# High weights of layer 1's paired units, placed 64 bytes lower in four tiles of their own

## The chip, the cores and the metric

The kernel runs on one core of one Trainium2 chip. The metric is the device time of one execution in microseconds (us); a run gives one time, and the median of several runs is compared.

A core has five engines that matter here: TensorE (PE in the profile, with its weight loads as PEld), VectorE (DVE), ScalarE (ACT), GpSimd (POOL) and SyncE (SP), which issues most of the DMA transfers. They run side by side and meet at semaphores. Data is worked on in a memory of 128 partitions; a tile takes the same bytes of each partition, and its address is the byte at which it starts there. A matmul has a stationary operand of 128 columns (the weights), which is loaded into the array first, and a moving operand of up to 512 columns, which streams past it.

## The reference

Two layers of a transformer-like mixer on 256 latent and 256 context tokens, 2048 features wide, in float32:

```python
for l in range(DEPTH):                                   # DEPTH = 2
    shift, scale, gate = jnp.split(silu_c @ w_mod[l] + b_mod[l], 3, axis=-1)
    h = rmsnorm(x, g_pre[l]) * (1.0 + scale[:, None]) + shift[:, None]
    h_c = rmsnorm(ctx, g_pre[l]) * (1.0 + scale_c) + shift_c
    proj, proj_c = h @ w_in[l], h_c @ w_in[l]
    y = mixer_branches(proj, latent_attn, ...)           # gMLP, attention, Fourier, each with a gate
    x_new = x + gate[:, None] * rmsnorm(y @ w_out[l], g_post[l])
    if not last:
        ...                                              # the same for the context
```

`w_in[l]` is 2048 by 5120 and `w_out[l]` 2048 by 2048. The second layer needs of the context only the keys and values, since only the latent tokens are returned.

## The kernel before

**Float32 in two parts.** Each operand of a large matmul is split into a high part (a cast to the type float32r) and a low part (the rest). A product of two operands is then three matmuls: high by high, high by low, low by high (`mm3`, L575).

**The stream of weights.** The weights come in chunks of 128 partitions by 1024 float32, 4096 bytes on each partition. The class `Stream` (L471) lists them in the order of use. For each one, SP issues the load into a tile `raw` (a ring of three), ACT casts it to `whi` (L544) and DVE writes the rest to `wlo` (L546). Both `whi` and `wlo` are rings of four tiles: the allocator gives the next chunk a tile whose last reader is done, and the cast waits for that reader. The stream runs three chunks ahead of the matmuls (`AHEAD`). Chunks that stand in `place` go to other tiles, and the two chunks of the unit `v` hold high and low parts of half a chunk in each tile (`twins`, L549).

**The units.** A unit is 128 columns of `w_in` by all 2048 rows: 16 blocks of 128 rows, in two chunks. In layer 0, `tunit` (L718) runs `mm3` for each block over the 512 columns of both streams of tokens. In layer 1 the tiles `hh` and `hl` hold, for latents and context in turn, high and low part side by side, 256 columns each. There `tunit1` (L742) runs a pair for each block (`mm2`, L730): the high weight against all 512 columns (L732), and the low weight against the 256 columns of the high part (L733). `joined` adds the two halves of the result. Units in pairs are `au2`, `au3`, `cx`, `ag`, `cg` (four each), `k` (two, each with both streams), `q` and `bg` (eight each); `av`, `au01` and `v` of layer 1 are worked in other ways.

**The order.** TensorE's instructions stand in the order in which the code issues them. Other work (attention, Fourier, the conditioning sums on DVE) is cut in steps and put between the matmuls by a planner of due times (`Later`). DVE, ACT and SP are ordered by a scheduler from priorities.

**Homes.** At the start `HOMES` (L93) creates one tile of every large tag in a fixed order, so that each has a fixed address; tags that aren't listed follow in the order of their first use. All homes but three at the start (`ct`, `cs`, `gs0`, 128 bytes each) and the last, `kt0`, take multiples of 512 bytes. `ones` is a tile of 128 by 128 ones; matmuls read up to 32 of its columns, and L1333 casts it all to a float32r tile for the last stage.

Of the kernel before, what the change touches and what calls it, by code (L numbers as in the profile page):

```python
# [7 lines left out]
F32 = mybir.dt.float32  # L8
F32R = mybir.dt.float32r
# [4 lines left out]
P = 128  # L14
D = 2048
KT = D // P
S = 256
# [49 lines left out]
def trunk_kernel(ctx: ExitStack, tc: tile.TileContext, xT, xhalf, cT, wss, wsl, wmod, win, wout0, wout1, const, vec, rows,  # L67
                 wmat, bs, sink, out):
    nc = tc.nc
    V, A, G, PE, DMA = nc.vector, nc.scalar, nc.gpsimd, nc.tensor, nc.sync  # L70
# [6 lines left out]
    def sb(shape, dt, tag, bufs=1):  # L77
        cnt[0] += 1
        return pool.tile(shape, dt, tag=tag, bufs=bufs, name=f"{tag}_{cnt[0]}")

    def w2k(shape, dt=F32):
        return sb(shape, dt, "w2k", W2K)
# [5 lines left out]
    def ms_ps(name="ms"):  # L88
        cnt[0] += 1
        return psum.tile([P, 512], F32, tag="ms", bufs=2, name=f"ps_{name}_{cnt[0]}")  # L90


    HOMES = ([("ct", 32, 1), ("cs", 32, 1), ("gs0", 32, 1)] + [(f"yy{i}", 1024, 1) for i in range(8)]  # L93
             + [("join", 256, 2), ("w2k", 512, W2K), ("mraw", 1024, 2)]
             + [(tag, 1024, n) for tag, n in (("macc", 1), ("vv", 1), ("raw", 3), ("whi", 4), ("wlo", 4), ("mg", 1), ("mgl", 1))]
             + [(f"{tag}{i}", 512, 1) for i in range(KT) for tag in ("hh", "hl")]
             + [(tag, 512, 1) for tag in ("acc", "ctrh", "ctrl", "nstrh", "nstrl", "ws", "bsb", "kt1")]
             + [("identr", P, 1), ("ones", P, 1), ("red", P, 2), ("m0r", P, 1), ("rbs", S, 2), ("kt0", 2 + KT * 32, 1)])
    for tag, n, bufs in HOMES:
        sb([P, n], F32, tag, bufs)  # L100

# [9 lines left out]
    ct = sb([P, KT, 2], F32, "ct")  # L111
    vecs = sb([P, 2, NVEC], F32, "vecs")
    cst = sb([P, NKEEP - P], F32, "cst")
    ones = sb([P, P], F32, "ones")
    V.memset(ones, 1.0)
    mhalf8 = sb([P, 8], F32, "mhalf")
    mhalf = mhalf8[:, 0:4]
# [19 lines left out]
    class low:  # L137


        def __init__(self, n):  # L140
            self.n = n
# [16 lines left out]
    identr = sb([P, P], F32R, "identr")  # L158
# [5 lines left out]
    gg0 = sb([P, KT, 2], F32, "gg0")  # L164
# [223 lines left out]
    state = {"ctx": [], "phase": "", "owed": 0.0}  # L388
# [43 lines left out]
    class Later:  # L432
# [19 lines left out]
        def flush(self):  # L452
# [6 lines left out]

    OUT = list(range(8, KT)) + list(range(8))  # L460
    NHI, NLO, NRAW = 4, 4, 3
    TAIL = [(("hl0 hl1", 1), ("hl2 hl3", 1)), (("hl4 hl5", 1), ("hl6 hl7", 1)),
            (("mraw", 2), ("mraw", 2)), (("macc", 1), ("ws bsb", 1)),
            (("yy4", 1), ("yy5", 1)), (("yy6", 1), ("yy7", 1))]
# [6 lines left out]
    class Stream:  # L471
        AHEAD = 3

        def __init__(self):
            self.src, self.out, self.pos, self.stop = [], [], 0, 0
            self.raws, self.rest = [], []
            self.place, self.behind, self.twin = {}, {}, set()
            for l in range(2):
                def half(name, i, h):
                    return win[l, UIDX[name][i], h]  # L480
                for i in range(2):
                    a = [half("av", 2 * i, 0), half("au01", i, 0), half("av", 2 * i, 1),
                         half("av", 2 * i + 1, 0), half("au01", i, 1), half("av", 2 * i + 1, 1)]
                    if l == 0:
                        a.insert(3 - i, half("au2", 0, i))
                        self.place[len(self.src) + 3 - i] = AU2[i]
                    self.src += a
                for i, u in enumerate(UNITS):
                    if u[0] not in ("av", "au01") + ("au2",) * (l == 0):
                        if u[0] == "v":  # L490
                            self.twin.update((len(self.src), len(self.src) + 1))
                        self.src += [win[l, i, 0], win[l, i, 1]]
                if l == 0:
                    self.src += [wout0[j, i] for j in OUT for i in range(2)]
                else:
                    self.src += [wout1[c, i] for c in range(4) for i in range(8)]
                if l == 0:
                    n = len(self.src) - 2 * HELD
                    self.place[n] = (("mraw", 2), ("mraw", 2))
                    self.place[n + 1] = (("macc", 1), ("mg", 1))  # L500
            for i, tags in enumerate(TAIL):
                self.place[len(self.src) - len(TAIL) + i] = tags
            self.raw_place = {len(self.src) - len(TAILRAW) + i: tags for i, tags in enumerate(TAILRAW)}
# [16 lines left out]
        def load_rest(self):  # L520
            n, r = self.rest.pop(0)
            DMA.dma_start(r[:, 512:], self.src[n][:, 512:])

        def emitting(self, cut=1024):

            if len(self.raws) == len(self.out):
                self.load()
            n = len(self.out)
            r = self.raws[n]
            if n in self.twin:  # L530
                yield from self.twins(r)
                return
            tags = self.place.get(n, (("whi", NHI), ("wlo", NLO)))
            hi, lo = ([sb([P, 1024 // len(t[0].split())], F32R, tag, t[1]) for tag in t[0].split()] for t in tags)
            self.out.append((hi, lo))
            cut = min(cut, 1024 // max(len(hi), len(lo), len(r) if isinstance(r, list) else 1))
            for i in range(0, 1024, cut):
                c = slice(i, i + cut)
                ph, pl = part((hi, lo), c)
                rc, _ = part((r, r), c)  # L540
                with ExitStack() as after:
                    for i in self.behind.get(n, ()):
                        after.enter_context(tc.issue_after(i.ins))
                    A.copy(ph, rc)  # L544
                yield
                self.last = V.tensor_tensor(out=pl, in0=rc, in1=ph.bitcast(F32), op=ALU.subtract)  # L546
                yield

        def twins(self, r):  # L549

            self.out.append([sb([P, 2, 2, 256], F32R, tag, n) for tag, n in (("whi", NHI), ("wlo", NLO))])
            for i, t in enumerate(self.out[-1]):
                rc = r[:, i * 512:(i + 1) * 512].rearrange("p (k c) -> p k c", c=256)
                A.copy(t[:, :, 0], rc)
                yield
                self.last = V.tensor_tensor(out=t[:, :, 1], in0=rc, in1=t[:, :, 0].bitcast(F32), op=ALU.subtract)
                yield
# [22 lines left out]
    def part(w, c):  # L580

        def of(t):
            if not isinstance(t, list):
                return t[:, c]
            n = t[0].shape[-1]
            return t[c.start // n][:, c.start % n:c.start % n + c.stop - c.start]

        return of(w[0]), of(w[1])
# [724 lines left out]
    def finish():  # L1313
# [16 lines left out]
        later.add(turn(), YT)  # L1330
        state["phase"] = "out1"
        state["ones"] = sb([P, P], F32R, "join", 2)
        A.copy(state["ones"], ones)  # L1333
        sums = sb([P, 2, 4], F32, "sums")
        gy = {}
        tot = sb([P, 2], F32, "tot")
# [65 lines left out]
    rbs = {}  # L1402
# [89 lines left out]
    with tc.manual_schedule(engines={EN.PE}):  # L1492
# [5 lines left out]
        raw = w2k([P, NFIRST])  # L1498
# [5 lines left out]
        for i in range(KT):  # L1504
# [12 lines left out]
            for a in range(2):  # L1517
                k = 2 * j + a
# [14 lines left out]
        for h, ps in enumerate((ms_ps("rs"), mm_ps("rs"))):  # L1533
            for j in range(2):
                c = slice(h * S + j * P, h * S + (j + 1) * P)
# [31 lines left out]
        state["acc"] = out_proj()  # L1567
        layer(1)
        finish()


# [75 lines left out]
```

## Time and profile before

| | us |
|---|---|
| three runs: median (lowest to highest) | 1119.2 (1117.8 to 1120.15) |
| the profiled execution | 1119.12 |
| its span, first to last instruction | 1117.3 |
| PE busy in the span | 1107.5 |
| layer 0, up to the pairs (0 to 763.6) | 763.6 |
| layer 1's units in pairs (763.6 to 1016.9) | 253.3 |
| layer 1's output projection and end (1016.9 to 1117.3) | 100.4 |

The granted clock of TensorE was 1.0 of full speed in nearly the whole span. The part up to 763.6 us holds the first matmuls of layer 1 (`av`, `au01`) too. A row of the timeline gives start, length, engine, line, operation, and output and inputs by tile names; the length of a matmul reaches past the start of the next, because matmuls are pipelined, so the distance from start to start is what one costs. A row of the table by stage gives its length, each engine's busy time with the number of its instructions, the granted clock, and the share and rate of the DMA engines.

### The profile page before, as it was taken

How to read it: one execution, taken by the hardware profiler on the slowest of the kernel's cores; microseconds unless marked ns; L12 is line 12 of the kernel's file. 1: busy time of each engine (PE TensorE's matmuls, PEld its weight loads, DVE VectorE, ACT ScalarE, POOL GpSimd, SP SyncE). 2: the span in 40 equal slices, each digit the busy share in tenths (PEclk: the TensorE clock that was granted, in tenths of full speed). 3: DMA queues.
4: the chain of work that ended last, by engine and by line, in shares of the span. 5: the costliest groups of instructions: out<-in, count | busy, mean ns of one | idle time of the engine just before them, and what ended most of it. 6: DMA issues, size and time to landing. Idle time of an engine off the chain costs nothing. (4 is left out here: it accounts for less than half of the span.)

```text
span 1117.3 us, 17365 instructions
## 1 busy us (share of the span) xinstructions
PE 1107.5 (99%) x6450; PEld 927.7 (83%) x6453; DVE 926.3 (83%) x1616; ACT 550.4 (49%) x1049; POOL 33.4 (3%) x43
## 2 busy tenths in 40 slices
PE   8999999999999999999999999999999999999998
PEld 4777888888888888888888888988888888888886
DVE  3677599999988897988988989396989789878874
ACT  4455823322235666622533324266665379867552
POOL 1000000000000000000000000030500000000000
PEclk9999999999999999999999999999999999999999
DMA  9999664566655343465556665385956686465981
GB/s 377 414 413 409 220 202 159 190 220 225 196 190 180 99 157 114 147 201 174 166 191 206 216 217 188 94 202 193 235 168 203 214 289 194 160 181 195 306 261 75
DMA packets 75525, 235.89 MB, mean 211 GB/s; under 512 B 8480, under 2 KB 15024, under 8 KB 75440
## 3 DMA queue, kind: packets, MB, share of 16 engines
q1 hardware_dynamic: 71088, 230.31, 61.5%
q0 software_dynamic: 4064, 3.69, 2.2%
q8 instruction: 50, 0.82, 0.3%
q10 hardware_dynamic: 288, 0.79, 0.2%
q14 instruction: 35, 0.29, 0.1%
HBM read 232.65 MB, written 2.10 MB: 210 GB/s over the span
## 5 line engine op out<-in xcount | busy, mean ns | idle before, releaser
L544 ACT CAST whi<-raw 128x1024 fp32r<-128x1024 f32 (+1 forms) x210 | 216.7, 1035 | 305.8 <-PE ps_t L577 203.7
L576 PE MATMUL ps_t<-hh,whi 128*128 128x512 f32 (+1 forms) x752 | 290.5, 386 | 0.0
L577 PE MATMUL ps_t<-hl,whi 128*128 128x512 f32 (+1 forms) x752 | 289.7, 385 | 0.0
L578 PE MATMUL ps_t<-hh,wlo 128*128 128x512 f32 (+1 forms) x752 | 289.6, 385 | 0.0
L546 DVE TENSOR_TENSOR wlo<-raw,whi 128x1024 fp32r<-128x1024 f32 (+1 forms) x210 | 250.9, 1198 | 43.2 <-ACT whi L544 38.7
L319 DVE SCALAR_TENSOR_TENSOR macc<-mraw,cs,macc 128x512 f32<-128x512 f32 x360 | 251.1, 744 | 13.4 <-DMA mraw<-in_wmod_dram 12.8
L732 PE MATMUL ps_t<-hh,whi 128*128 128x512 f32 x512 | 184.4, 399 | 0.0
L578 PEld LDWEIGHTS ps_t<-hh,wlo 128*128 128x128 f32 x752 | 141.3, 188 | 28.7
L576 PEld LDWEIGHTS ps_t<-hh,whi 128*128 128x128 f32 x752 | 141.4, 188 | 27.0
L577 PEld LDWEIGHTS ps_t<-hl,whi 128*128 128x128 f32 x752 | 141.4, 188 | 26.2
L733 PE MATMUL ps_t<-hh,wlo 128*128 128x256 f32 x512 | 143.0, 279 | 0.0
L732 PEld LDWEIGHTS ps_t<-hh,whi 128*128 128x128 f32 x512 | 96.3, 188 | 21.2
L733 PEld LDWEIGHTS ps_t<-hh,wlo 128*128 128x128 f32 x512 | 96.6, 189 | 0.4
L576 PE MATMUL ps_y<-whi,hh 128*128 128x512 f32 x104 | 41.3, 397 | 0.0
L578 PE MATMUL ps_y<-whi,hh 128*128 128x512 f32 x104 | 40.6, 390 | 0.0
L577 PE MATMUL ps_y<-wlo,hh 128*128 128x512 f32 x104 | 40.5, 390 | 0.0
L593 ACT CAST w2k<-ps_tp 128x512 fp32r<-128x512 f32 x40 | 23.3, 584 | 21.3 <-PE ps_scc L577 13.7
L594 DVE TENSOR_TENSOR w2k<-ps_tp,w2k 128x512 fp32r<-128x512 f32 x40 | 27.4, 684 | 3.7 <-ACT w2k L593 2.4
L606 POOL TENSOR_TENSOR rs_b<-rs_a,mhalf 128x2 f32<-128x2 f32 (+1 forms) x7 | 6.3, 897 | 753.0 <-DVE mx L1422 583.1
L1156 ACT ACTIVATE w2k<-w2k,den 128x512 f32<-128x512 f32 (+1 forms) x48 | 28.2, 646 | 0.7 <-DVE den L1151 0.6
L811 PE MATMUL ps_av<-whi,hh 128*128 128x512 f32 x64 | 24.3, 395 | 0.2 <-ACT hh L681 0.2
L576 PE MATMUL ps_o<-w2k,vv 128*128 128x256 f32 x80 | 24.5, 306 | 0.0
(493 smaller groups left out, 1820.6 us busy)
## 6 DMA issues: line engine op xcount, KB each, us to landing
raw<-in_win_dram SPq DMA_DIRECT2D x158, 512.0 KB, 4.3
mraw<-in_wmod_dram SPq DMA_DIRECT2D x128, 512.0 KB, 4.4
raw<-in_wout_dram SPq DMA_DIRECT2D x60, 512.0 KB, 4.5
mraw<-in_wsl_dram SPq DMA_DIRECT2D x12, 512.0 KB, 7.2
yy<-in_xhalf_dram SPq DMA_DIRECT2D x7, 512.0 KB, 7.4
mg<-in_wsl_dram SPq DMA_DIRECT2D x7, 512.0 KB, 8.7
mgl<-in_wsl_dram SPq DMA_DIRECT2D x7, 512.0 KB, 9.2
yy<-in_xhalf_dram POOLq DMA_DIRECT2D x28, 128.0 KB, 7.6
```

The costliest lines, as they stand in the source:

```text
L319: V.scalar_tensor_tensor(out=acc[:, s], in0=w[:, kk % 2], scalar=c, in1=acc[:, s], op0=ALU.mult, op1=ALU.add)
L544: A.copy(ph, rc)
L546: self.last = V.tensor_tensor(out=pl, in0=rc, in1=ph.bitcast(F32), op=ALU.subtract)
L576: PE.matmul(ps, st[0], mv[0], start=start, stop=False)
L577: PE.matmul(ps, st[0], mv[1], start=False, stop=False)
L578: PE.matmul(ps, st[1], mv[0], start=False, stop=stop)
L593: A.copy(hi, src)
L594: V.tensor_tensor(out=lo, in0=src, in1=hi.bitcast(F32), op=ALU.subtract)
L732: PE.matmul(ps, w[0], h, start=k == 0, stop=False)
L733: PE.matmul(ps[:, 0:S], w[1], h[:, 0:S], start=False, stop=k == KT - 1)
L811: PE.matmul(ps, st[a], mv[b], start=start and (a, b) == (0, 0), stop=stop and (a, b) == (1, 0))
L1156: A.activation(prob[i][:, b * w:(b + 1) * w], prob[i][:, b * w:(b + 1) * w], AF.Copy, scale=den[:, c:c + 1])
```

## The change

The ring of four `whi` tiles becomes four tiles with tags of their own, `whi0` to `whi3`, each of 1040 elements, 16 (64 bytes) more than a chunk. A chunk of a paired unit of layer 1 starts at the beginning of its tile; every other chunk starts 16 elements further. Which of the four tiles a chunk gets was up to the allocator; it now follows from a list, `highs`, in which the first is taken and put at the end, or the second at eight places (`OVERTAKEN`) where the ring had done so. To make room and to set the addresses, the four tiles stand near the end of the homes, each behind a small tile of 32 elements and two of 4, and `ones` shrinks to 32 columns; its cast at L1333 reads one column 128 times.

```diff
+    ASIDE = 16
     HOMES = ([("ct", 32, 1), ("cs", 32, 1), ("gs0", 32, 1)] + [(f"yy{i}", 1024, 1) for i in range(8)]
              + [("join", 256, 2), ("w2k", 512, W2K), ("mraw", 1024, 2)]
-             + [(tag, 1024, n) for tag, n in (("macc", 1), ("vv", 1), ("raw", 3), ("whi", 4), ("wlo", 4), ("mg", 1), ("mgl", 1))]
+             + [(tag, 1024, n) for tag, n in (("macc", 1), ("vv", 1), ("raw", 3), ("wlo", 4), ("mg", 1), ("mgl", 1))]
...
-             + [("identr", P, 1), ("ones", P, 1), ("red", P, 2), ("m0r", P, 1), ("rbs", S, 2), ("kt0", 2 + KT * 32, 1)])
+             + [("identr", P, 1), ("red", P, 2), ("m0r", P, 1), ("rbs", S, 2)])
+    for i, (tag, small) in enumerate((("gs1", "es"), ("sh0", "mx"), ("sh1", "nm"), ("gg0", "den"))):
+        HOMES += [(tag, 32, 1), (small, 4, 2), (f"whi{i}", 1024 + ASIDE, 1)]
+    HOMES += [("kt0", 2 + KT * 32, 1)]
...
-    ones = sb([P, P], F32, "ones")
+    ones = sb([P, 32], F32, "ones")
...
+    OVERTAKEN = 5, 8, 11, 14, 113, 116, 119, 122
...
-            self.place, self.behind, self.twin = {}, {}, set()
+            self.place, self.behind, self.twin, self.aside, self.nhi = {}, {}, set(), set(), 0
+            self.highs = list(range(NHI))
...
                         if u[0] == "v":
                             self.twin.update((len(self.src), len(self.src) + 1))
+                        elif l:
+                            self.aside.update((len(self.src), len(self.src) + 1))
...
+        def high(self, aside=False):
+            i = self.highs.pop(1 if self.nhi in OVERTAKEN else 0)
+            self.highs.append(i)
+            self.nhi += 1
+            o = 0 if aside else ASIDE
+            return sb([P, 1024 + ASIDE], F32R, f"whi{i}")[:, o:o + 1024]
...
-            tags = self.place.get(n, (("whi", NHI), ("wlo", NLO)))
-            hi, lo = ([sb([P, 1024 // len(t[0].split())], F32R, tag, t[1]) for tag in t[0].split()] for t in tags)
+            tags = self.place.get(n, (None, ("wlo", NLO)))
+            hi, lo = ([sb([P, 1024 // len(t[0].split())], F32R, tag, t[1]) for tag in t[0].split()] if t
+                      else [self.high(n in self.aside)] for t in tags)
...
-            self.out.append([sb([P, 2, 2, 256], F32R, tag, n) for tag, n in (("whi", NHI), ("wlo", NLO))])
+            self.out.append([t.rearrange("p (k a c) -> p k a c", k=2, a=2) for t in (self.high(), sb([P, 1024], F32R, "wlo", NLO))])
...
-        A.copy(state["ones"], ones)
+        A.copy(state["ones"], ones[:, 0:1].to_broadcast([P, P]))
```

## The prediction, made before the changed kernel ran

> **What bounds the kernel now.** I read the page first, for the engine that has no room left, then the table of busy time by stage, then the waits of TensorE, and last the starts of single instructions in the timeline.
>
> ```profile
> span 1117.3 us, 17365 instructions
> PE 1107.5 (99%) x6450; PEld 927.7 (83%) x6453; DVE 926.3 (83%) x1616; ACT 550.4 (49%) x1049; POOL 33.4 (3%) x43
> ```
>
> TensorE is busy for 99% of the span. The change touches layer 1's units in pairs, which run from 763.6 to 1016.9 us, so this is the stage to look at (columns of the table: length, then busy time and count of PE, PEld, DVE, ACT and POOL, then the granted clock and the DMA engines).
>
> ```profile
> 763.60:824.70 61.10, 61.06 (x372) 53.94 (x371) 50.27 (x107) 39.55 (x87) 17.40 (x19) 1.00 0.74 204
> 824.70:907.90 83.20, 83.20 (x482) 72.75 (x481) 69.52 (x126) 44.41 (x84) 0.00 (x0) 1.00 0.71 232
> 907.90:1016.90 109.00, 109.00 (x659) 96.28 (x658) 92.29 (x178) 86.01 (x177) 0.00 (x0) 1.00 0.58 184
> ```
>
> PE has no idle time here, at the full clock. What TensorE waited for between 120 and 1017 us are these two waits alone (total, times, longest):
>
> ```profile
> PE ps_f L1082 <- DVE w2k L594: 0.3, 1, 0.3
> PE ps_av L577 <- DVE wlo L546: 0.2, 1, 0.2
> ```
>
> So no semaphore holds PE back: the stage lasts as long as its matmuls follow each other. What a pair costs is therefore not in a wait but in the distance from one start to the next. The two lines of a pair:
>
> ```profile
> L732 PE MATMUL ps_t<-hh,whi x512: 387/395/481, 763.7 to 1016.5; 128*128 128x512 f32 x171
> L732 PE MATMUL ps_t<-hl,whi x32: 395/395/395, 852.8 to 874.3; 128*128 128x512 f32 x32
> ```
>
> That is 512 + 32 = 544 pairs: 32 units of 16 rows of weights, and 32 more for the context half of the two k units. Each is a matmul of 512 columns with the high weight (L732), then one of 256 columns with the low weight (L733). The durations (395 ns) overlap, so I take starts. The timeline at the first matmul of four units (start, us, engine, line):
>
> ```profile
> 824.73 0.39 PE L732 MATMUL ps_t<-hh,whi 128*128 128x512 f32 x1
> 824.96 0.27 PE L733 MATMUL ps_t<-hh,wlo 128*128 128x256 f32 x1
> 825.07 0.40 PE L732 MATMUL ps_t<-hh,whi 128*128 128x512 f32 x1
> ...
> 852.46 0.39 PE L732 MATMUL ps_t<-hh,whi 128*128 128x512 f32 x1
> ...
> 999.89 0.40 PE L732 MATMUL ps_t<-hh,whi 128*128 128x512 f32 x1
> 1000.12 0.28 PE L733 MATMUL ps_t<-hh,wlo 128*128 128x256 f32 x1
> 1000.24 0.40 PE L732 MATMUL ps_t<-hh,whi 128*128 128x512 f32 x1
> ...
> 1011.20 0.40 PE L732 MATMUL ps_t<-hh,whi 128*128 128x512 f32 x1
> ```
>
> From 824.73 to 852.46 run five units, 80 pairs, and nothing else: 27.73 / 80 = 346.6 ns a pair. From 999.89 to 1011.20 run two units, 32 pairs: 11.31 / 32 = 353.4 ns. **The same instructions have two rhythms, 6.8 ns apart**, with no wait listed in either. I next ask what 6.8 ns is. Matmuls in threes, with 512 and with 256 columns (28 threes lie between the last two rows):
>
> ```profile
> 300.21 0.39 PE L576 MATMUL ps_t<-hh,whi 128*128 128x512 f32 x1
> ...
> 300.89 0.39 PE L576 MATMUL ps_t<-hh,whi 128*128 128x512 f32 x1
> ...
> 705.34 0.28 PE L576 MATMUL ps_t<-hh,mraw 128*128 128x256 f32 x1
> ...
> 715.42 0.28 PE L576 MATMUL ps_t<-hh,whi 128*128 128x256 f32 x1
> ```
>
> One matmul of 512 columns takes 0.68 / 3 = 227 ns, one of 256 takes 10.08 / 84 = 120 ns. The difference of 107 ns over 256 columns makes 0.417 ns a column, so 16 columns, which are 64 bytes of float32 on each partition, take 6.7 ns. The rhythms differ by about one such granule in each pair. And 512 columns need 213 ns of their own, 256 need 107: every matmul here pays 13 ns, two granules, over its columns.
>
> **The change part by part.**
>
> *The place of the high weights (L533, L551 of the kernel before, and the homes at L93).* All homes ahead of these tiles add up to multiples of 512 bytes from one to the next, so weights and moving columns begin on the same 128-byte boundary today. After the change a tile of 1040 elements begins 128 + 2 x 32 = 192 bytes past such a boundary (one small tile of 32 elements and two of 4, each of which takes 32 bytes). A paired unit of layer 1 starts at its beginning, which is 64 past a multiple of 128; every other unit starts 16 elements on, at a multiple of 128. What it costs hangs on what PE does when a weight load and the moving columns read side by side. The high weight of a pair is loaded while the 256 columns of the pair before stream. A load by itself is bounded by the transposes, where one load and 128 short columns make a step (first a row of the timeline, then the shortest, median and longest duration of all 160):
>
> ```profile
> 361.66 0.60 PE L1176 MATMUL ps_tp<-identr,w2k 128*128 128x128 f32 x4
> ```
>
> ```profile
> L1176 PE MATMUL ps_tp<-identr,w2k x160: 270/272/273, 361.7 to 991.6; 128*128 128x128 f32 x160
> ```
>
> Four of them last 0.60 us and one 0.272, so a step is (0.60 - 0.27) / 3 = 0.11 us, close to the 107 ns of 256 columns. In this step of a pair load and columns are thus equally long, and together they take 110 to 120 ns in the rows above: neither has spare time, and an offset between their boundaries can decide who gives way. No trace shows an fp32 load off a 128-byte boundary against a stream of 256 columns, so I bound it. The best case is that pairs cost their columns alone: 768 x 0.417 = 320 ns, 27 to 33 ns less, 544 x 30 = 16.3 us. The worst is that a 512-byte load off its boundary covers five stretches of 128 bytes instead of four: 0.11 x 5/4 = 0.137 us, about 20 ns over today's step, 544 x 20 = 10.9 us more. The nearest rows against the worst are the loads for the conditioning sums, 32 columns that begin 8 past a 128-byte boundary and on one in turn:
>
> ```profile
> 24.11 0.51 PE L211 MATMUL ps_mod<-mg,kt 128*32 128x128 f32 x12
> 24.44 0.62 PE L211 MATMUL ps_mod<-mgl,kt 128*32 128x128 f32 x16
> ```
>
> Twelve, in three groups of four, take 0.33 us: 0.11 a group, no more than the aligned transposes. I take **one granule saved in each pair**: the two rhythms show that it is the unit in which the streams yield to each other, and the step with the high load has 0 to 11 ns above its floor of 109 in which to save it. 544 x 6.7 = 3.6 us.
>
> [...]
>
> *The ring in four tiles (`high`, `highs`, `OVERTAKEN`).* The places that the 214 tiles of the old ring have in the program before, followed in order, are those that the new list gives, with the names of two tiles exchanged. So each cast still waits for the same matmul. No instruction or DMA is added, and no queue is moved past. If the order slipped, the cover is this: the casts already wait for PE to give a tile back.
>
> ```profile
> ACT whi L544 <- PE ps_t L732: 22.3, 21, 2.4
> ```
>
> A slip by one tile would delay a cast by a unit's half, some 2.8 us, and PE holds three tiles ahead; I cost it at nothing.
>
> *What follows sooner.* If PE saves 3.6 us in 253 us, DVE must do its work in less. Its tightest stage is the last of the table: 92.3 us busy of 109.0. With 14 units, 224 pairs, PE would save 1.5 us there, and 15 us of DVE's idle time remain. ACT has 23 us left there. So nothing else becomes late.
>
> *The `ones` tile, 128 columns to 32, and its broadcast copy at L1333.*
>
> ```profile
> L1333 ACT CAST join<-ones x1: 302/302/302, 1019.0 to 1019.0; 128x128 fp32r<-128x128 f32 x1
> ```
>
> It still writes 128 columns; reading one of them again and again should take the same 0.3 us, on an ACT that is half idle. Zero. The small tiles that move (`es`, `mx`, `nm`, `den`, `gs1` and the like) hold at most 32 elements: zero.
>
> The sum is 1117.3 - 3.6 = 1113.7 us of span. This profiled execution took 1119.12 us, 1.8 us more than its span, and the median is 1119.2, the same to 0.1. I forecast **1115.6 us**.
>
> **The rivals.**
>
> *Only the slow rhythm goes.* The 176 pairs between 824.7 and 907.9 keep 346.6 ns, and the others reach it. These are 368; after each foreign matmul their rhythm is set anew, and I put three quarters of them in the slow one: 276 x 6.8 = 1.9 us, 1117.3. For it: the quick rhythm is one that the kernel already has. Against it: it needs the shift to help exactly where it is slow.
>
> *Nothing happens.* If loads and columns never meet in memory, the 13 ns are a fixed price of changing weights and the rhythms come from how instructions are issued: 1119.2. For it: the step of 512 columns pays the same 13 ns as that of 256, though it has twice the time for its load. That the order slips, so that the change is not what it says, costs nothing by the bound above and gives the same time.
>
> *It goes slower.* The mechanism: load and columns have already settled into the order that today's common boundary allows, and a load shifted by half of 128 bytes meets the columns one granule later each time. Place: the second step of each of the 544 pairs. Price: 6.7 ns, 3.6 us, 1122.8. It decides as soon as that step goes over 120 ns. The same sign has the rule of five stretches for four, 1130.1, against which the sums' groups speak. Half of the ordinary units also come to lie 256 bytes past a multiple of 512, which no row of this kernel shows for weights; I see no sign that it matters, since weights at all eight column offsets of 512 bytes have the same steps.
>
> *It goes much better.* The second step falls to its floor of 109 and the first loses its surplus too: 13 ns or more a pair, 7.3 us, 1111.9.
>
> **How the numbers follow.** About 0.2% (2.2 us) is what a measurement of this kernel can tell from no change. One granule less in each pair: 0.42. Much better: 0.06. Only the slow rhythm: 0.12, of which a sixth comes out beyond 0.2%. Nothing: 0.19. Slower by a granule or a part of it: 0.17; by the five stretches: 0.04. So faster 0.42 + 0.06 + 0.02 = 0.50, same 0.10 + 0.19 = 0.29, slower 0.21. The range runs from 1112.0, where the better case lies on the edge, to 1122.0, which takes in half of the slower one; about 0.17 is left out. The forecast's own range is 1114.5 to 1116.9.
>
> **What would show it.** Right: five units with nothing between take under 27.5 us instead of 27.73, by L733-to-L732 steps of 105 to 113 ns, and the first matmul of the output projection starts some 3.6 us before 1016.85; layer 0's threes keep 0.68 us. Wrong: pairs stay at 346.6 and 353.4 (nothing), all at 346.6 (rhythm), or the second step is over 120 (slower). A new PE wait on `whi` or `wlo` would mean that the ring's order was not kept.

## The result, and the profile after

The changed kernel takes **1115.89 us** (median of eight runs, 1115.31 to 1117.02) against 1118.74 us for the kernel before (eight runs, 1117.80 to 1120.15): a ratio of 0.9973, with an interval of 0.9964 to 0.9983. It is 2.85 us faster. The profiled execution took 1116.08 us.

The page of the changed kernel, first the span and the busy times:

```profile
span 1114.3 us, 17364 instructions
PE 1104.2 (99%) x6450; PEld 926.6 (83%) x6453; DVE 925.9 (83%) x1616; ACT 550.4 (49%) x1049; POOL 33.3 (3%) x43
```

The span is 3.0 us shorter, and PE's busy time is 3.3 us shorter for the same 6450 matmuls. No other engine's time moved by more than 0.4 us except PEld's, by 1.1. In the changed kernel the lines of a pair are L748 and L749 (before, L732 and L733), those of `mm3` L592 to L594, and the split on DVE is L610. The timeline shows where the 3.0 us lie (start, us, engine, line):

```profile
763.48 0.40 PE L748 MATMUL ps_t<-hh,whi 128*128 128x512 f32 x1
...
823.85 0.39 PE L748 MATMUL ps_t<-hh,whi 128*128 128x512 f32 x1
...
829.29 0.39 PE L748 MATMUL ps_t<-hh,whi 128*128 128x512 f32 x1
829.52 0.28 PE L749 MATMUL ps_t<-hh,wlo 128*128 128x256 f32 x1
829.63 0.39 PE L748 MATMUL ps_t<-hh,whi 128*128 128x512 f32 x1
...
851.05 0.39 PE L748 MATMUL ps_t<-hh,whi 128*128 128x512 f32 x1
...
872.81 0.40 PE L1250 MATMUL ps_v<-whi,hh 128*128 128x512 f32 x1
...
895.42 0.40 PE L748 MATMUL ps_t<-hh,whi 128*128 128x512 f32 x1
...
901.02 0.40 PE L748 MATMUL ps_t<-hh,whi 128*128 128x512 f32 x1
...
1013.85 0.40 PE L592 MATMUL ps_y<-whi,hh 128*128 128x512 f32 x1
```

The same marks in the trace of before:

```profile
763.69 0.40 PE L732 MATMUL ps_t<-hh,whi 128*128 128x512 f32 x1
...
874.64 0.39 PE L1234 MATMUL ps_v<-whi,hh 128*128 128x512 f32 x1
...
896.83 0.39 PE L732 MATMUL ps_t<-hh,whi 128*128 128x512 f32 x1
...
902.38 0.39 PE L732 MATMUL ps_t<-hh,whi 128*128 128x512 f32 x1
...
1016.85 0.40 PE L576 MATMUL ps_y<-whi,hh 128*128 128x512 f32 x1
```

Read them in four steps.

- *Layer 0 is unchanged.* The first pair starts 0.2 us earlier, and from the first matmul of the output projection to the end of the span both kernels need 100.4 or 100.5 us. The stage of the pairs went from 253.16 us (1016.85 - 763.69) to 250.37 us: 2.79 of the 3.0 us.
- *The five units with nothing between* take 851.05 - 823.85 = 27.20 us instead of 27.73: 340.0 ns a pair instead of 346.6. Within a pair, the step from L748 to L749 is now 0.23 us and the step back 0.11.
- *The unit `v`* (64 pairs, whose high weights were not shifted) became slower: 895.42 - 872.81 = 22.61 us, 353.3 ns a pair, instead of 22.19 us, 346.7 ns.
- *The first `q` unit behind `v`* takes 901.02 - 895.42 = 5.60 us, 350 ns a pair, where it took 902.38 - 896.83 = 5.55 us before, and the second `q` unit goes from 5.54 to 5.60 us. Two units that were shifted became slower: not every shifted unit reached 340.

Over all pairs with no other matmul next to them, taken from every start in the timeline, the mean went from 350.1 ns (233.9 for the step of 512 columns, 116.2 for that of 256) to 342.5 (228.3 and 114.1). The sum of the steps over the whole stage, after less before, is:

| | us |
|---|---|
| the matmuls of the pairs | -3.99 |
| `v` | +0.42 |
| attention, `ps_o` | +0.54 |
| attention, `ps_sc` | +0.11 |
| pairs with other work between | +0.20 |
| the rest | -0.07 |
| the stage | -2.79 |

The waits show the attention's part. What TensorE's matmuls waited for between 120 us and 1014 us (total, times, longest), then its weight loads from 763.6 to 1013 us, both of the changed kernel:

```profile
PE ps_mix L1054 <- issue: 0.3, 1, 0.3
PE ps_f L1098 <- DVE w2k L610: 0.2, 1, 0.2
```

```profile
PEld ps_mix L1054 <- issue: 0.5, 1, 0.5
PEld ps_sc L594 <- DVE w2k L610: 0.4, 1, 0.4
PEld ps_o L593 <- DVE w2k L610: 0.3, 1, 0.3
PEld ps_sc L592 <- ACT w2k L609: 0.2, 1, 0.2
```

The wait of `ps_o` and that of `ps_sc` on ACT are new: of the attention's loads, only one of `ps_sc` waited in the trace of before (the other two waits listed there are on `issue`):

```profile
PEld ps_sc L578 <- DVE w2k L594: 0.3, 1, 0.3
```

The instructions at the wait of `ps_o`, in the changed kernel:

```profile
945.69 0.68 DVE L610 TENSOR_TENSOR w2k<-ps_tp,w2k 128x512 fp32r<-128x512 f32 x1
945.91 0.36 PE L592 MATMUL ps_o<-w2k,vv 128*128 128x256 f32 x1
946.43 0.39 PE L593 MATMUL ps_o<-w2k,vv 128*128 128x256 f32 x1
```

and in the kernel before:

```profile
947.03 0.68 DVE L594 TENSOR_TENSOR w2k<-ps_tp,w2k 128x512 fp32r<-128x512 f32 x1
947.53 0.36 PE L576 MATMUL ps_o<-w2k,vv 128*128 128x256 f32 x1
947.77 0.39 PE L577 MATMUL ps_o<-w2k,vv 128*128 128x256 f32 x1
```

DVE writes the low part of `w2k` until 946.37. TensorE now gets there 1.62 us sooner than before, DVE's step only 1.34 us sooner, and the second matmul starts 0.52 us after the first instead of 0.24. This one step is about half of the 0.54 us of `ps_o`.

### The profile page after: what moved, and what is told of

Read it like the earlier page. It is cut to its first block, busy times and chain, and to the rows that moved or that the text cites. A ratio compares the mean times of both kernels' runs of the same rounds, so it can differ in the third digit from the quotient of the medians.

```text
span 1114.3 us, 17364 instructions
## 1 busy us (share of the span) xinstructions
PE 1104.2 (99%) x6450; PEld 926.6 (83%) x6453; DVE 925.9 (83%) x1616; ACT 550.4 (49%) x1049; POOL 33.3 (3%) x43
## 5 line engine op out<-in xcount | busy, mean ns | idle before, releaser
L592 PE MATMUL ps_t<-hh,whi 128*128 128x512 f32 (+1 forms) x752 | 290.6, 386 | 0.0
L594 PE MATMUL ps_t<-hh,wlo 128*128 128x512 f32 (+1 forms) x752 | 289.6, 385 | 0.0
L748 PE MATMUL ps_t<-hh,whi 128*128 128x512 f32 x512 | 180.8, 393 | 0.0
L594 PEld LDWEIGHTS ps_t<-hh,wlo 128*128 128x128 f32 x752 | 141.3, 188 | 28.5
L592 PEld LDWEIGHTS ps_t<-hh,whi 128*128 128x128 f32 x752 | 141.4, 188 | 26.8
L749 PE MATMUL ps_t<-hh,wlo 128*128 128x256 f32 x512 | 142.0, 277 | 0.0
L748 PEld LDWEIGHTS ps_t<-hh,whi 128*128 128x128 f32 x512 | 96.3, 188 | 19.0
L749 PEld LDWEIGHTS ps_t<-hh,wlo 128*128 128x128 f32 x512 | 96.2, 188 | 0.4
L592 PE MATMUL ps_y<-whi,hh 128*128 128x512 f32 x104 | 41.3, 397 | 0.0
L594 PE MATMUL ps_y<-whi,hh 128*128 128x512 f32 x104 | 40.6, 390 | 0.0
L610 DVE TENSOR_TENSOR w2k<-ps_tp,w2k 128x512 fp32r<-128x512 f32 x40 | 27.4, 685 | 3.0 <-ACT w2k L609 2.0
L592 PE MATMUL ps_o<-w2k,vv 128*128 128x256 f32 x80 | 24.5, 306 | 0.0
```

The costliest lines, as they stand in the source:

```text
L592: PE.matmul(ps, st[0], mv[0], start=start, stop=False)
L594: PE.matmul(ps, st[1], mv[0], start=False, stop=stop)
L610: V.tensor_tensor(out=lo, in0=src, in1=hi.bitcast(F32), op=ALU.subtract)
L748: PE.matmul(ps, w[0], h, start=k == 0, stop=False)
L749: PE.matmul(ps[:, 0:S], w[1], h[:, 0:S], start=False, stop=k == KT - 1)
```

## The experiments

All are edits of the changed kernel, and each computes the whole reference. "The columns" are `hh` and `hl`. An offset is where the high weights begin relative to the columns, in bytes and apart from whole multiples of 256 bytes: 0 before, -64 for the pairs after. ASIDE counts elements of 4 bytes. `padA` and `padB` are tiles of 64 bytes that nothing uses; each moves all tiles behind it. Means are of the pairs with no other matmul next to them; "threes" are layer 0's units and its output projection, three matmuls of 512 columns for each block of rows. Experiments 1 and 2 and the second kernel of 7 were run several times; every other kernel ran once, and its numbers are those of one execution. Where a diff shows added lines alone, the lines that they replace are left out.

**1. Without the shift.** The four tiles, their order, the small homes and `ones` stay; all chunks begin at the higher place.

```diff
-            o = 0 if aside else ASIDE
+            o = ASIDE
```

> The changed kernel, but every chunk's high weights start 16 elements into their tile, the paired units' too: the homes, the four tiles, their order and the small ones tile stay, the 64 bytes go. If the 64 bytes between the high weights and the columns next to them are the cause, the pairs of the five units with nothing between them go back from 340 to 346.6 or 353.4 ns (27.7 us or more for 80 pairs) and the time is 1118.7 within 0.6. If the other parts of the change were the cause (new places, a list for the ring), the pairs keep 340 ns and the time is 1115.9.

Measured: 1118.62 us (eleven runs, 1118.04 to 1119.74) against 1118.61 before, a ratio of 1.000 (0.9991 to 1.0009). The pairs take 350.3 ns, the five units 851.38 - 823.65 = 27.73 us:

```profile
823.65 0.39 PE L748 MATMUL ps_t<-hh,whi 128*128 128x512 f32 x1
...
851.38 0.39 PE L748 MATMUL ps_t<-hh,whi 128*128 128x512 f32 x1
```

So the whole gain is the 64 bytes; everything else in the diff costs or brings no more than the 0.1% of that interval. This kernel issues the same instructions in the same order as the changed one on PE, DVE, ACT and SP, and in it `ps_o` takes as long as before (+0.02 us). The longer waits of the attention therefore come of PE being early, not of an order that changed.

**2. All chunks shifted**, layer 0's and the output projections' too.

```diff
-            o = 0 if aside else ASIDE
+            o = 0
```

> All chunks in the four tiles start at the tile's beginning, 64 past a multiple of 128 bytes, so layer 0's threes (two of their three loads are high weights) and the matmuls that stream high weights are shifted too. If each load beside a stream off its boundary saves a granule of 6.7 ns, a three of 512 columns falls from 680 ns to 667 or 673 and the 752 threes of layer 0 give 5 to 10 us: 1106 to 1111. If a stream of 512 columns hides the load whatever its place, the threes stay at 680 ns and the time at 1115.9. If a shift can also cost a granule, threes go to 687 or 693 ns and the time to 1121 to 1126.

Measured: 1122.47 us (1121.97 to 1123.32), ratio 1.0036 (1.0023 to 1.0048). The pairs gain as in the changed kernel (342.2 ns; the five units 27.20 us). The threes lose: 687.9 ns instead of 682.1. One unit of 16 threes:

```profile
521.94 0.39 PE L592 MATMUL ps_t<-hh,whi 128*128 128x512 f32 x1
...
532.93 0.39 PE L592 MATMUL ps_t<-hh,whi 128*128 128x512 f32 x1
```

That is 10.99 us; a unit of threes on the common boundary takes 10.88 (experiment 5). **The place that is best for pairs is worse for threes**, by 5.8 ns for each three, about the granule of 6.7 ns that I had estimated.

**3. The low weights.** `padA` ahead of the ring of `wlo` and `padB` behind it put the low weights of all units 64 bytes lower against the columns: with the high weights of the pairs at -64 too, and with them at 0.

```diff
-             + [(tag, 1024, n) for tag, n in (("macc", 1), ("vv", 1), ("raw", 3), ("wlo", 4), ("mg", 1), ("mgl", 1))]
+             + [(tag, 1024, n) for tag, n in (("macc", 1), ("vv", 1), ("raw", 3))]
+             + [("padA", 16, 1), ("wlo", 1024, 4), ("padB", 16, 1), ("mg", 1024, 1), ("mgl", 1024, 1)]
```

and in the second of the two also

```diff
-            o = 0 if aside else ASIDE
+            o = ASIDE
```

> The changed kernel with the low weights 64 bytes past a multiple of 128 too, in all units (a filler of 64 bytes ahead of their ring and one behind it). In the pairs both loads are now off the columns' boundary, and high and low weights are in step with each other. If what matters is a load against the columns that stream beside it, each pair loses a second granule: 333 ns, 26.7 us for 80 pairs. If what matters is high against low weights, the old rhythms of 346.6 and 353.4 ns come back. Threes of layer 0 have one load in three shifted: 680 ns if they do not care, 673 or 687 if they do.

> As the run with both, but the high weights all start at a multiple of 128: only the low weights are shifted. By load against columns the load beside the 512 columns is now off and the one beside the 256 is not; if that long stream has room for its load anyway, the pairs keep 346.6 or 353.4 ns, and if each load counts alike they take 340. By high against low weights, 340 ns as in the changed kernel.

Measured: 1129.3 and 1130.11 us (one run each; before 1118.61). The five units of pairs took 861.08 - 832.82 = 28.26 us with both shifted (353.3 ns a pair) and 28.00 us with the low ones alone (350.0); the threes took 693.6 ns in both. So the gain needs the high weights to be off the columns **and** the low weights on their boundary; two loads that are off in the same way bring the slow rhythm.

**4. Is it a place in memory, or the distance between two?** In the first kernel `padA` (without the `padB` behind the low weights) lifts low weights and columns by 64 bytes, `padB` ahead of the four tiles lifts these by 64 more, and all chunks take the higher place. I meant this as -64; counted in 256 bytes it is **+64**.

```diff
+             + [("padA", 16, 1), ("wlo", 1024, 4), ("mg", 1024, 1), ("mgl", 1024, 1)]
...
+              + [("identr", P, 1), ("red", P, 2), ("m0r", P, 1), ("rbs", S, 2), ("padB", 16, 1)])
...
+            o = ASIDE
```

> All high weights start at a multiple of 128 bytes, and everything that the pairs read beside them is shifted instead: the low weights and the columns (hh, hl) start 64 past one. Seen from the high weights this is the changed kernel again. If the place of one read against the other is what counts, the pairs have 340 ns (227 and 113), and layer 0's threes 688 ns as in the run with all high weights low. If a read off its own 128-byte boundary is what counts, the pairs behave like no run so far, with low weights and columns both off: over 346 ns.

Measured: 1131.13 us (before 1118.34), five units 862.76 - 834.76 = 28.00 us, threes 697.5 ns. No gain: either the place itself counts, or the sign does. Two more kernels tell these apart. One leaves the columns where they were and puts the pairs alone at +64; the other lifts low weights and columns by 64 and leaves all high weights at -64 from them.

```diff
+              + [("identr", P, 1), ("red", P, 2), ("m0r", P, 1), ("rbs", S, 2), ("padA", 16, 1)])
...
+    HOMES += [("padB", 16, 1), ("kt0", 2 + KT * 32, 1)]
...
+            o = ASIDE if aside else 0
```

```diff
+             + [("padA", 16, 1), ("wlo", 1024, 4), ("mg", 1024, 1), ("mgl", 1024, 1)]
...
+    HOMES += [("padB", 16, 1), ("kt0", 2 + KT * 32, 1)]
...
+            o = 0
```

> The paired units' high weights start 64 bytes above the boundary of 128 (and of 256) instead of 64 below; all else lies as in the changed kernel. If places repeat every 128 bytes, above and below are the same: pairs of 340 ns, 227 and 113, and a span near 1114. If the sign counts (a period of 256, or a load that must come before the columns), the pairs have some other rhythm, between 340 and 353 ns, and the span lies between 1114 and 1117.

> The run with low weights and columns shifted once more, but with the high weights 64 bytes below them up to 256, where the first lay 64 above up to 256. If only distances count, with a period of 256, the pairs now have 340 ns; with a period of 128 they would have had it in the first. If the place against a fixed boundary counts as well, they stay a mixture around 348 ns.

Measured: 1118.61 and 1123.19 us (before 1118.73). The five units of pairs at +64:

```profile
823.98 0.39 PE L748 MATMUL ps_t<-hh,whi 128*128 128x512 f32 x1
...
851.98 0.39 PE L748 MATMUL ps_t<-hh,whi 128*128 128x512 f32 x1
```

and at -64 with the columns lifted:

```profile
828.51 0.39 PE L749 MATMUL ps_t<-hh,whi 128*128 128x512 f32 x1
...
855.71 0.39 PE L749 MATMUL ps_t<-hh,whi 128*128 128x512 f32 x1
```

28.00 us (350.0 ns) at +64, 27.20 us (340.0 ns) at -64, the changed kernel's own value though columns and low weights lie elsewhere; its threes lose as in experiment 2 (688.7 ns). **What counts is the distance between high weights and the other two, and its sign.** The threes show the sign most plainly: 688 ns at -64, 697.5 at +64. In the pairs the quick rhythm is not missing at +64, but rare. Eight pairs in a row in the kernel with the pairs alone at +64:

```profile
993.32 0.39 PE L748 MATMUL ps_t<-hh,whi 128*128 128x512 f32 x1
...
996.04 0.39 PE L748 MATMUL ps_t<-hh,whi 128*128 128x512 f32 x1
```

That is 2.72 us, 340 ns a pair. Of 443 pairs with no other matmul next to them, 62 take at most 341 ns in this kernel and 104 in the first one of this experiment; 306 do so at -64 with the columns lifted, 340 in the changed kernel, and 2 in experiment 1. So the offset shows in how often the pairs run in the quick rhythm, and a stretch of five units says less than the mean: 342.5 ns at -64 in the changed kernel, 349.1 at +64.

Since -64 and +64 are 128 apart and differ in this way, the pattern repeats at no less than 256 bytes, not at the 128 that I had taken. At -64 it does repeat at 256: neighbouring tiles of the four begin 4352 bytes (17 x 256) apart, so that, counted in 512 bytes, the chunks of the pairs lie at -64 or at +192, and each of the ten chunks of the five units of the changed kernel takes 2.72 us.

**5. How sharp is it?** The offset goes by unit, in one kernel: -64, -48, -32, -16 for the pairs, and 0, -64, -48, -32, -16 for layer 0's threes. A second kernel reaches further, with tiles of 24 elements more: -96, -80, -64 for the pairs and 0, -96, -80, -16 for the threes.

```diff
+                            o = (0, 4, 8, 12)[i % 4] if l else (16, 0, 4, 8, 12)[i % 5]
+                            self.aside.update({len(self.src): o, len(self.src) + 1: o})
```

```diff
+    ASIDE = 24
...
+                            o = (0, 4, 8)[i % 3] if l else (24, 0, 4, 20)[i % 4]
```

> The high weights' start against a multiple of 128 bytes goes around from unit to unit: -64, -48, -32, -16 in layer 1's pairs, 0, -64, -48, -32, -16 in layer 0's threes. If there are two positions alone, each of 64 bytes, -48 behaves like -64 and -16 and -32 are a mixture of stretches or like 0: pairs of 340 or 346 to 353 ns. [...] If any start off a multiple of 64 bytes costs a further read for each load, -48, -32 and -16 are slower than both, 353 ns and more. Threes: 681 ns at 0 and 688 at -64; the others by the same reading.

> High weights further down: in layer 1's pairs -96, -80 and -64 bytes in turn, in layer 0's threes 0, -96, -80 and -16; the rest as in the changed kernel. If a pair is shortest where its high load trails by a quarter of a period of 256 bytes, -64 keeps 340 ns and -80 and -96 are longer by a part of a granule, as -48 was (347). If it only had to trail by 64 or more, -80 and -96 have 340 ns too. If less is possible, one of them comes to 333. Threes: 681 at 0, over 688 elsewhere.

Measured: 1121.33 us (before 1118.34) and 1119.82 us (before 1118.73). In the first kernel units of pairs at -16, -64, -48 and -32 follow each other:

```profile
827.75 0.39 PE L748 MATMUL ps_t<-hh,whi 128*128 128x512 f32 x1
...
833.34 0.40 PE L748 MATMUL ps_t<-hh,whi 128*128 128x512 f32 x1
...
838.80 0.39 PE L748 MATMUL ps_t<-hh,whi 128*128 128x512 f32 x1
...
844.34 0.39 PE L748 MATMUL ps_t<-hh,whi 128*128 128x512 f32 x1
...
849.86 0.40 PE L748 MATMUL ps_t<-hh,whi 128*128 128x512 f32 x1
```

5.59, 5.46, 5.54 and 5.52 us: 349, 341, 346 and 345 ns a pair. And five units of threes, at 0, -64, -48, -32 and -16:

```profile
499.91 0.39 PE L592 MATMUL ps_t<-hh,whi 128*128 128x512 f32 x1
...
510.79 0.39 PE L592 MATMUL ps_t<-hh,whi 128*128 128x512 f32 x1
...
521.78 0.40 PE L592 MATMUL ps_t<-hh,whi 128*128 128x512 f32 x1
...
532.88 0.39 PE L592 MATMUL ps_t<-hh,whi 128*128 128x512 f32 x1
...
544.07 0.39 PE L592 MATMUL ps_t<-hh,whi 128*128 128x512 f32 x1
...
555.24 0.40 PE L592 MATMUL ps_t<-hh,whi 128*128 128x512 f32 x1
```

10.88 us at 0, 10.99 at -64, 11.10 at -48, 11.19 at -32 and 11.17 at -16. The means over all undisturbed pairs and threes, in ns, with the kernel each comes from:

| offset, bytes | pair | three |
|---|---|---|
| -96 | 349.3 (second scan) | 693.9 (second) |
| -80 | 349.5 (second) | 690.5 (second) |
| -64 | 342.5 (changed kernel), 342.6 (first scan), 343.4 (second) | 687.9 (experiment 2), 688.1 (first) |
| -48 | 347.3 (first) | 693.6 (first) |
| -32 | 345.9 (first) | 698.4 (first) |
| -16 | 349.2 (first) | 692.1 (first), 683.2 (second) |
| 0 | 350.1 (before), 350.3 (experiment 1) | 682.2 (before), 681.3 (first) |
| +64 | 349.1 (experiment 4, pairs alone) | 697.5 (experiment 4, first kernel) |

In the mean, a move of 16 bytes either way from -64 loses most or all of the gain: -64 is the best of the places tried, and a narrow one. No other place is better than 0 for the threes. The two values at -16 do not agree. A unit of threes at -16 in the second scan:

```profile
498.15 0.39 PE L592 MATMUL ps_t<-hh,whi 128*128 128x512 f32 x1
...
509.03 0.39 PE L592 MATMUL ps_t<-hh,whi 128*128 128x512 f32 x1
```

That is 10.88 us, as at 0, where the first scan had 11.17 us at -16: what a unit costs hangs on more than its own offset.

**6. Low weights at +64**, the other way round, by small tiles of 64 bytes ahead of them and 192 behind, with the pairs' high weights at -64 to 0 by unit.

```diff
+              + [("rs_a", 4, 2), ("wlo", 1024, 4)] + [(tag, 8, 1) for tag in ("mhalf", "zero8", "skb", "nskb", "sums")] + [("ss", 4, 1), ("mg", 1024, 1), ("mgl", 1024, 1)]
...
+                            o = (0, 4, 8, 12, 16)[i % 5] if l else (16, 0, 4, 8, 12)[i % 5]
```

> The low weights of all units 64 bytes above the columns (they were at 0 in the changed kernel, at -64 in two runs: worse both times), and high weights at -64, -48, -32, -16, 0 in pairs, 0, -64, -48, -32, -16 in threes. If a load wants to differ from the columns in the one direction only, the low load here costs as in those runs: pairs at 349 ns or more, threes over 688. If high and low loads want to lie apart by 64 bytes or more, pairs with high at 0 or -64 have 340 ns or less, and some threes fall under 680.

Measured: 1127.57 us (before 1118.73). No offset of the high weights brings 340 ns back: the means of all five lie between 347.7 and 352.4 ns, and the threes at 687.6 to 696 ns. Of the three places tried for the low weights (-64, 0, +64), the columns' boundary is the best: with the high weights at -64 the pairs took 353.3 ns when the low ones lay at -64 (the five units of experiment 3) and 342.5 when they lay at 0 (the changed kernel).

**7. The unit `v` and its neighbours.** `v` kept its place and yet became slower. One kernel shifts chunks of `au01` (first line) and `v` (second line, an offset for each layer and chunk) as well; another puts back the second chunk of `k1`, the 16 pairs ahead of `v`, to see whether `v` takes over the rhythm in which TensorE reaches it.

```diff
+                        self.aside.update({len(self.src) + 1: 0, len(self.src) + 4: 0})
...
+                            self.aside.update({len(self.src): (12, 4)[l], len(self.src) + 1: (8, 0)[l]})
```

```diff
-                            self.aside.update((len(self.src), len(self.src) + 1))
+                            self.aside.update((len(self.src), len(self.src) + (u[0] != "k1")))
```

> The changed kernel with the v units' high weights, which are streamed there, at -16 and -32 (layer 0) and -48 and -64 bytes (layer 1), and with layer 1's au01 at -64 too. In v it is the columns that move, against both loads; a v pair has 353 ns at 0 in both layers of the changed kernel. If a shift of one read against the other helps whichever of the two is moved, the half of layer 1's v at -64 falls to 340 ns and 32 pairs give 0.4 us. If both loads must not be off, as when high and low weights were shifted together (352 ns), it stays at 350 or over.

> The changed kernel, but the second chunk of unit k1 starts at a multiple of 128 bytes again: its 16 pairs are the last before unit v. Layer 1's v pairs took 346.7 ns before the change and 353 after it, though none of their reads lies otherwise against the others. If a rhythm is set by the matmuls just before, the 16 pairs go to 346 to 350 ns (0.1 to 0.2 us lost), v comes back to 346.7 (0.4 us won) and the two q units after it leave 350 ns for 340 or stay (0.3 us or nothing): 1115.2 to 1115.7. If v's 353 ns come from the new place of its own tile, v stays at 353 and the time is 1116.0.

Measured: 1115.08 us in one run (before 1118.73) for the first. In it `v` of layer 1 takes 352.5 ns at -48 and -64, no better than 353; `au01`'s pairs 346.9 ns, which were 345.8. Layer 0's `v`, at -16 and -32, did become quicker:

```profile
308.74 0.40 PE L1252 MATMUL ps_v<-whi,hh 128*128 128x512 f32 x1
...
331.12 0.39 PE L594 MATMUL ps_t<-hh,whi 128*128 128x512 f32 x1
```

That is 22.38 us; in the changed kernel it is 331.75 - 309.15 = 22.60. So moving the columns against both loads may help as well, in one run by 3.4 ns a pair. The time of this one run lies 0.23 us below the lowest of the changed kernel's eight, which spread over 1.7 us, so I do not count it as a gain. The second: 1116.53 us (ten runs, 1115.25 to 1117.35) against 1118.94, ratio 0.9975 (0.9966 to 0.9985), the same as the changed kernel. The pairs put back took 353.1 ns and `v` stayed at 353.5, so the question whether `v` inherits its rhythm was not answered: what came ahead of it was slow again. But behind it the `q` units, whose instructions and places are those of the changed kernel, took another rhythm:

```profile
895.87 0.39 PE L748 MATMUL ps_t<-hh,whi 128*128 128x512 f32 x1
...
901.31 0.39 PE L748 MATMUL ps_t<-hh,whi 128*128 128x512 f32 x1
...
906.75 0.39 PE L748 MATMUL ps_t<-hh,whi 128*128 128x512 f32 x1
```

5.44 us each, 340 ns a pair, where the changed kernel has 5.60. In the time this does not show, because TensorE waits elsewhere in the profiled execution:

```profile
PE ps_z L594 <- DVE w2k L610: 0.7, 1, 0.7
```

The matmuls into `ps_z` take 1.0 us more than in the changed kernel, and the stage of the pairs 0.9 us more. With experiment 1, in which `v` has the places of the changed kernel and takes 346.7 ns (895.76 - 873.57 = 22.19 us), this makes two cases in which **equal instructions at equal places run in different rhythms**, with no listed wait in either.

None of the twelve kernels is measurably faster than the changed one.

## Why the prediction was right, and where it was not

*The forecast: 3.6 us, one granule in each of 544 pairs.* What held is that the place of the high weights against the columns sets the rhythm, and that it moves by about a granule; that two reads yield to each other, as the prediction puts it, no row shows. The quick rhythm lost one granule (346.6 to 340.0, 6.6 ns), the slow one two (353.4 to 340.0, 13.4), and two `q` units went the other way, from about 346.7 to 350. The pairs' matmuls saved 3.99 us, where one granule in each made 3.6. The 1115.6 us forecast and the 1115.89 measured agree in part by luck: more was saved in the pairs and about 1.2 us was lost beside them, and the forecast started from 1119.2 us, the median of three runs, where eight give 1118.74. The saving was 2.85 us, not 3.6.

*The step that was named was the wrong one.* I had the saving in the second step, where the load of the high weight and the 256 columns are equally long, and called its floor 109 ns. The second step fell by 2.1 ns on average (116.2 to 114.1), the first by 5.6 (233.9 to 228.3). So 5.6 of the 7.6 ns, about three quarters, came from the step of 512 columns, which in the quick rhythm now lasts what each matmul of a three does (227 ns). That 512 columns leave twice the time for a load (213 ns against 107, by my estimate of 0.417 ns a column) was my argument for "nothing happens"; it does not protect the step.

*"So nothing else becomes late" was wrong*, by 0.5 to 0.7 us. I compared DVE's busy time with a whole stage of 109 us. But the attention is a chain of short steps between PE and DVE inside that stage, and there PE waits, in the rows above because it came 0.28 us too early, however idle DVE is elsewhere: `ps_o` +0.54 us and `ps_sc` +0.11.

*Edits that I cost at nothing.* The ring in four tiles, the homes, `ones` and the small tiles: nothing, by experiment 1 (ratio 1.000). Not in my sum was `v`, 0.42 us slower without having moved.

*The rivals.* Only the slow rhythm goes (1117.3): no, the five units that had the quick one fell too. Nothing happens: the difference between experiment 1 and the changed kernel, 1118.62 against 1115.89, is the 64 bytes alone. The threes say the same: a unit of them takes 10.88 us at 0 and 11.19 at -32, in one kernel (experiment 5). Whether the read of the weights or that of the columns then waits for the other, the trace does not show. Slower by a granule: not for the pairs as a whole, but it came true for the threes as soon as they were shifted (experiment 2), and pairs with both weights shifted took 353.3 ns in the five units. The rule of five stretches for four falls: the pairs' mean is 342.5 ns at -64 and 349.1 at +64, and 350.1 on the boundary. The remark on tiles 256 bytes past a multiple of 512 held: the threes did not move (682.2 and 682.1 ns).

*What stays open.* The trace does not show the reads of weights and columns, so whether one of them gives way, which one, and why less at -64, was not seen. That the pattern repeats at 256 bytes is seen for pairs at -64 and threes at 0 alone, and offsets beyond -96 and +64, or between 0 and +64, were not tried. Most offsets were run once. What sets the rhythm of a unit after other matmuls, and so whether `v` could keep 346.7 and all pairs get 340, is not settled.

## What to carry to other kernels

Where TensorE is busy all the time and no wait is listed, take the distance from start to start of equal instructions at several places: if it has more than one value, the addresses of weights and columns relative to each other are worth a try, in steps of 16 bytes, for each pattern of matmuls by itself, because the best place for one pattern can be a loss for another (-64 brought the pairs from 350.1 to 342.5 ns and the threes from 682.1 to 687.9). Compare many stretches, because one offset has several rhythms (units of pairs at -64 ran at 340 and at 350 ns in one kernel). Try it with an offset inside a tile that is a little too large, so that nothing else moves, and keep a kernel with the larger tile and no offset as the control. And judge whether another engine becomes late at its tightest chain of steps, not by its share of a stage.

## What the runs showed of the hardware

- The time of a matmul that follows another with no wait hangs on where its weights lie relative to the moving columns: pairs 340 to 353 ns, threes 681 to 698 ns, a spread of 4% and 2.5%.
- The effect of an offset is narrow in the mean (pairs at -80: 349.5, -64: 342.5, -48: 347.3 ns) and has a sign (pairs at +64: 349.1; threes 688 at -64, 697.5 at +64), so it does not follow from 64-byte or 128-byte boundaries alone.
- It differs between the two patterns of matmuls: of the places tried, -64 is best for the pairs (342.5 ns, 350.1 at 0), and none is better than 0 for the threes (681.3 to 682.2 ns, 687.9 at -64).
- One stream of instructions has several steady rhythms (340, 346.7, 350 and 353.3 ns a pair) and can stay in one over 16 to 144 pairs (in the changed kernel 872.81 - 823.85 = 48.96 us, 340.0 ns a pair).
